# The tensor engine's products for an expert's slots beyond 128, under a compare-and-branch

## The chip, the cores and the metric

The kernel runs on one core of one Trainium2 chip. The metric is the device time of one execution in microseconds. Times are given as the median of three runs with the lowest and the highest beside it; the profile is one further execution, recorded by the hardware profiler.

The engines appear as the profile names them: PE is the tensor engine's matmul, PEld its weight load, DVE the vector engine, ACT the scalar engine, POOL GpSimd and SP the sync engine, which issues DMAs. A name with q at the end (ACTq, PEldq) is that engine's sequencer. PSUM is the memory in which PE accumulates.

## What is computed

The reference is two blocks of a language model, one after the other, on 512 tokens of 1024 values in fp32. The first block has two layers, and the second of them ends in a mixture of experts: eight experts of width 1536, two of them for each token.

```python
def moe_swiglu(h, router, w_gate, w_up, w_down):
    ...
    probs = jax.nn.softmax((ht @ router).astype(F32), axis=-1)
    top_p, top_i = lax.top_k(probs, TOP_K)
    top_p = top_p / jnp.sum(top_p, axis=-1, keepdims=True)
    ...
```

For each expert the tokens go through `silu(h @ w_gate) * (h @ w_up)` and then through `@ w_down`; a token's two results are added with the gates that the router gives. Here 512 tokens with two experts each make 1024 pairs, 128 for each of the eight experts on average; how many an expert really gets depends on the data. Everything else in the reference (the mixers, the dense feed-forward, the second block with its attention over a memory) is untouched by the change.

## The kernel before

The kernel is one program for all stages. A scheduler of the framework puts the instructions of a stage in an order for each engine and adds the semaphore waits that the data need; the source order around a stage is only its input. The stage in question is `moe` (line 1996), which runs from about 1063 to 1665 us of the profiled execution.

Ahead of it `dispatch` (line 1842) counts the tokens of each expert and gives each token its slots. An expert has `CAP` = 160 slots: 128 first ones, and 32 more for what goes beyond 128. A flag tells whether any expert has over 160; then, at the end of the program, a dense second computation replaces the result (under an `If`, line 2353; it is skipped here).

For expert `e`, `fetch` (line 2004) gathers the rows of its tokens with two indirect DMAs of POOL, `xa` (128 rows) and `xb` (32 rows). `turn` (line 2011) transposes them on PE. The 128 tokens are split in a high and a low part, `xh` and `xl`; the other 32 stay whole in `xs`.

Weights come in pieces through `weights` (line 2028). SP issues the DMA of a piece into `raw`, a ring of 8 buffers, ACT copies it to a rounded high part `wh`, and DVE subtracts to get the low part `wl`. A piece of the first product (gate and up) is 128×1536 fp32, 768 KB, and there are eight for each of two halves of an expert. A piece of the second product (down) is 128×1024, 512 KB, and there are twelve.

`block` (line 2036) does the 128 tokens for one piece with three products in a faster format: high by high, high by low, low by high. `few` (line 2045) does the other 32 tokens. It is called after every fourth piece (`FEW` = 4) and multiplies `xs` by the weights as loaded (`raw`), in fp32, four pieces at a time, with 16 matmuls in four groups of 32 columns of the array, into a PSUM tile `sec`. I call these 16 matmuls a section. In the trace a matmul in fp32 stands as two records, so a section is 32 records. A half (`gu`, line 2054) has two sections, a down product (`down`, line 2098) three: seven for an expert, 56 in all.

After the down product ACT and DVE copy the result out of PSUM into `y` (128 rows) and `ys` (the section's 32), and ACT's queue writes them to `ye` in memory, with one large transfer (line 2116) and four small ones (line 2118). After the last expert, indirect DMAs of POOL gather the rows of `ye` into `ya` and `yb` (line 2122). The hidden values are transposed for the down product by `turn_hid` (line 2079), with parts `th`, `tl` for the 128 tokens and `tsec` for the 32.

The loop of the stage runs over the experts: first half of expert e, down product of expert e-1, second half of expert e. The transposes are called from inside the loops over pieces, so that PE has them between matmuls.

The scheduler decides where a section stands in PE's stream. It spreads a section's matmuls between those of `block`, or puts them in one run.

Of the kernel before, what the change touches and what calls it, by code (L numbers as in the profile page):

```python
# [12 lines left out]
I32 = mybir.dt.int32  # L13
U32 = mybir.dt.uint32
AF = mybir.ActivationFunctionType
ALU = mybir.AluOpType
# [5 lines left out]
DFF, DFE, NE = 2816, 1536, 8  # L22
# [262 lines left out]
class Net:  # L285
# [72 lines left out]
    def sm(self, name, n):  # L358
        return self.M.tile([128, n], F32, name=name, tag="s_" + name, bufs=1)
# [1461 lines left out]
    def moe_init(self):  # L1821
        self.hd = self.D.tile([T, D], F32, name="hd")
        self.ye = self.D.tile([NE * CAP, D], F32, name="ye")
        self.flag = self.C.tile([1, 1], I32, name="flag")
        self.slot = self.C.tile([128, 2, 4], I32, name="slot")
        self.tokens = self.C.tile([128, 2, 8], I32, name="tokens")
        self.rp = self.C.tile([128, 2, 3, 4], F32, name="rp")
# [14 lines left out]
    def dispatch(self):  # L1842

        nc, F = self.nc, self.F
        tt, ts = nc.vector.tensor_tensor, nc.vector.tensor_scalar
        M_ = ALU.mult
        g = self.p("L1.n2")
        self.xg = []

        def chunk(c):  # L1850
            x = self.t("xg", "h")
            ts(x, self.X[c], g[:, c:c + 1], None, op0=M_)
            self.xg.append(x)
            F.set(0.6, "xg", c)

        sel, gates, r, _ = yield from self.route(g, lambda c: F.event("X", c), chunk)
        self.hrms = r
        sm, rp = self.rsm, self.rp

        pre, tot, fl = sm(4, 8), sm(8), sm(2)  # L1860
        nc.vector.memset(pre[:, 0], 0.0)
        for n in range(1, 4):
            tt(pre[:, n], pre[:, n - 1], sel[:, n - 1], op=ALU.add)
        tt(tot, pre[:, 3], sel[:, 3], op=ALU.add)
        yield F.event("sel")
        yield "px"
        pr = self.ps("px")
        pst = pr[:, 32:40]
        pr = pr[:, 0:32].rearrange("p (n e) -> p n e", n=4)
        self.pe.matmul(pr, self.const("tri128"), sel, start=True, stop=False)  # L1870
        self.pe.matmul(pr, self.const("ones"), pre, start=False, stop=True)
        self.pe.matmul(pst, self.const("ones"), tot, start=True, stop=True)
        st = sm(3, 4, 8)
        tt(st[:, 0], pr, sel, op=ALU.subtract)
        tt(st[:, 1], st[:, 0], self.const("ecap")[:, None, :].to_broadcast([128, 4, 8]), op=ALU.add)
        nc.vector.tensor_copy(st[:, 2], gates)

        big = self.t("rbig", "u")[:, :256].rearrange("p (n e f) -> p n e f", n=4, e=8)
        lt = self.const("lt8").rearrange("p (e f) -> p e f", e=8)[:, None].to_broadcast([128, 4, 8, 8])
        tt(big, sel[:, :, None, :].to_broadcast([128, 4, 8, 8]), lt, op=M_)  # L1880
        cnt, m, pk, ok = sm(4, 8), sm(4, 8), sm(3, 4, 8), sm(2, 4)
        nc.vector.tensor_reduce(cnt, big, axis=AX, op=ALU.add)
        at = self.t("slots", "u")[:, :CAP]
        nc.scalar.dma_start(at, self.A["slots"])
        oh, tid = [], []
        for k in range(2):
            ts(m, cnt, float(k), None, op0=ALU.is_equal)
            tt(m, m, sel, op=M_)
            tt(pk, st, m[:, None].to_broadcast([128, 3, 4, 8]), op=M_)
            nc.vector.tensor_reduce(rp[:, k], pk, axis=AX, op=ALU.add)  # L1890
            tid.append(sm(4, 8))
            tt(tid[k], m, self.const("tok")[:, :, None].to_broadcast([128, 4, 8]), op=M_)
            oh.append(self.t("oh", "B", (128, 4, CAP)))
            tt(oh[k], at[:, None, :].to_broadcast([128, 4, CAP]), rp[:, k, 0, :, None].to_broadcast([128, 4, CAP]),
               op=ALU.is_equal)
        F.rel("px", 2.0)
        yield 5.0
        yield "px"
        pi = self.ps("px")
        for o, w, c in ((0, 128, 0), (128, 32, 8)):  # L1900
            for q in range(8):
                k, n = q // 4, q % 4
                self.pe.matmul(pi[0:w, c:c + 8], oh[k][:, n, o:o + w], tid[k][:, n], start=q == 0, stop=q == 7)
        nc.vector.tensor_copy(self.tokens[:, 0], pi[:, 0:8])
        nc.vector.tensor_copy(self.tokens[0:32, 1], pi[0:32, 8:16])
        F.rel("px", 0.5)

        ts(ok, rp[:, :, 0], float(CAP), None, op0=ALU.is_lt)
        tt(ok, rp[:, :, 1], ok, op=M_)
        nc.vector.tensor_copy(self.slot, ok)  # L1910
        nc.vector.tensor_reduce(fl[:, 0:1], pst, axis=AX, op=ALU.max)
        ts(fl[:, 1:2], fl[:, 0:1], float(CAP), None, op0=ALU.is_gt)
        nc.vector.tensor_copy(self.flag, fl[0:1, 1:2])

    def rows(self):

# [79 lines left out]
    def moe(self, xin):  # L1996

        nc, A = self.nc, self.A
        ident = self.const("ident")
        tt, ts, act = nc.vector.tensor_tensor, nc.vector.tensor_scalar, nc.scalar.activation  # L2000
# [27 lines left out]
        def weights(src, n):  # L2028
            raw = self.t("raw", "rw", (128, 1536))[:, :n]
            hi, lo = (self.t(k, k, (128, 1536), F32R)[:, :n] for k in ("wh", "wl"))  # L2030
            nc.sync.dma_start(raw, src)
            self.wmark = act(hi, raw, AF.Copy)  # L2032
            tt(lo, raw, hi.bitcast(F32), op=ALU.subtract)  # L2033
            return raw, hi, lo
# [7 lines left out]
                self.pe.matmul(p, ah, lo[:, s], start=False, stop=False)  # L2042
                self.pe.matmul(p, al, hi[:, s], start=False, stop=last)

        def few(sec, todo, first, last):

            for i, (as_, raw) in enumerate(todo):
                q = raw.shape[1] // 4
                for b in range(4):
                    self.pe.matmul(sec[32 * b:32 * b + 32], as_, raw[:, q * b:q * b + q],  # L2050
                                   start=first and i == 0, stop=last and i == len(todo) - 1,
                                   tile_position=(0, 32 * b), skip_group_check=True)
            todo.clear()

        def gu(e, half, x, at=None):
            hi, lo, xs = x
            pg = [self.ps("pm")[:, :384] for _ in range(2)]
            pu = [self.ps("pf")[:, :384] for _ in range(2)]
            sec = self.ps("pf")[:, :384]
            todo = []  # L2060
            for k in range(8):
                w = weights(A["s_gu"][e, half, k], 1536)
                block(pg + pu, (hi[:, k], lo[:, k], xs[:, k]), w, 384, k == 0, k == 7)
                todo.append((xs[:, k], w[0]))
                if k % self.FEW == self.FEW - 1:
                    few(sec, todo, k < self.FEW, k == 7)
                if at and k in at:
                    at[k]()
            hid = self.t("hid", "hid", (128, 2, 384))
            for b in range(2):  # L2070
                sg = self.t("msg", "sg", (128, 384))
                act(sg, pg[b], AF.Silu)
                tt(hid[:, b], pu[b], sg, op=M_)
            hs, sg = self.t("hs", "hs", (128, 384)), self.t("msg", "sg", (128, 384))
            act(sg[64:128], sec[0:64], AF.Silu)
            tt(hs[64:128], sec[64:128], sg[64:128], op=M_)
            return hid, hs
# [21 lines left out]
        def down(e, T_, at=None):  # L2099
            th, tl, tsec = T_  # L2100
            ts_ = tsec.rearrange("p h b c s -> p (h b c) s")
            py, sec = [self.ps("px") for _ in range(2)], self.ps("px")[:, :256]
            todo = []
            for f in range(12):
                w = weights(A["s_dn"][e, f], D)
                block(py, (th[:, f], tl[:, f], ts_[:, f]), w, 512, f == 0, f == 11)
                todo.append((ts_[:, f], w[0]))
                if f % self.FEW == self.FEW - 1:
                    few(sec, todo, f < self.FEW, f == 11)
                if at and f in at:  # L2110
                    at[f]()
            y, ys = self.t("y", "y", (128, D)), self.t("ys", "ys", (128, 256))
            act(y[:, 0:512], py[0], AF.Copy)
            nc.vector.tensor_copy(y[:, 512:D], py[1])
            nc.vector.tensor_copy(ys, sec)
            nc.scalar.dma_start(self.ye[e * CAP:e * CAP + 128], y)
            for b in range(4):
                nc.scalar.dma_start(self.ye[e * CAP + 128:e * CAP + 160, 256 * b:256 * b + 256],
                                    ys[32 * b:32 * b + 32])
# [7 lines left out]
        for e in range(NE):  # L2127
            last = T_
# [253 lines left out]
```

## Time and profile before

| quantity | value |
|---|---|
| median of 3 runs | 2693.75 us |
| lowest and highest | 2688.41 and 2696.49 us |
| the profiled execution | 2687.84 us, its span 2686.1 us |
| PE busy over the span | 2560.9 us, 95% |
| DVE, ACT, POOL busy | 59%, 42%, 14% |
| mean DMA rate over the span | 134 GB/s |

The span is the time from the first to the last recorded instruction; the execution's own time is a little longer. Busy shares are means over stages with different limits. In the table of slices of the page, the slices of the mixture stage show PE at nine tenths or more nearly throughout, and DMA at seven to eight tenths, where most of the rest of the program has two or three. The parts to look at for this change are the stretches of that stage, single sections in the timeline, the landings of DMAs, and the places where PE stands.

### The profile page before, as it was taken

Reading aid. Unit: us, or ns where it says so; the run is one execution under the profiler, and the core shown is the slowest. Engines: PE = TensorE matmul, PEld = TensorE weight load, DVE = VectorE, ACT = ScalarE, POOL = GpSimd, SP = SyncE. Lnnn points to the kernel's source line nnn. Section 1 sums busy time; section 2 is a strip of 40 time slices with the busy share of each in tenths; the row PEclk is TensorE's granted clock in tenths of the full one; section 3 lists DMA queues with packets and bytes.
Section 4 is the critical chain, followed back from the end, with each engine's and each line's share of the span. In section 5 each row is a group of like instructions: output and inputs, shape, how many; then the busy total and the mean of one; then the engine's idle time right before and its main releaser. Section 6 shows DMA issues by size and latency. Waiting matters only on the chain.

```text
span 2686.1 us, 44080 instructions
## 1 busy us (share of the span) xinstructions
PE 2560.9 (95%) x18168; PEld 2012.0 (75%) x18168; DVE 1577.1 (59%) x2276; ACT 1126.1 (42%) x1608; POOL 366.9 (14%) x291
## 2 busy tenths in 40 slices
PE   7899999999989998999999998899989999999998
PEld 6787788888868677877777776676666676788887
DVE  6856743434575655766766675666744644544445
ACT  5344422223434534655555554553322334433332
POOL 3331000000343302000000001233432000000000
PEclk9999999999999998999999999999989999999999
DMA  3111322222311226787777776323233422222221
GB/s 117 55 57 41 90 91 95 94 94 96 117 56 62 65 81 214 271 317 282 289 268 280 267 269 234 126 69 104 87 112 111 158 90 66 92 94 94 94 94 57
DMA packets 102321, 359.40 MB, mean 134 GB/s; under 512 B 12384, under 2 KB 17888, under 8 KB 102112
## 3 DMA queue, kind: packets, MB, share of 16 engines
q1 hardware_dynamic: 81504, 305.32, 33.1%
q0 software_dynamic: 8128, 27.27, 2.9%
q10 hardware_dynamic: 12480, 23.91, 2.5%
q8 instruction: 145, 2.38, 0.4%
q14 instruction: 64, 0.52, 0.1%
HBM read 331.28 MB, written 25.17 MB: 133 GB/s over the span
## 4 chain that ended last, share of the span: by engine, by line
PE 56%; DVE 7%; issue 3%; ACT 2%; DMA 2%; POOL 0%; ACTq 0%; DVEq 0%; POOLq 0%
PE pm L278 34%; PE px L278 11%; PE pf L278 10%; PE px L282 1%; DVE ipr L480 1%; DVE cy L677 0%; DVE G L1587 0%; PE pf L282 0%; DMA ye<-ys 0%; DVE wlo L400 0%; DMA ya<-ye,slot 0%; DVE Tl L481 0%; DMA yb<-ye,slot 0%; ACT whi L398 0%; DVE rk L1592 0%
## 5 line engine op out<-in xcount | busy, mean ns | idle before, releaser
L398 ACT ACTIVATE whi<-raw 128x1024 fp32r<-128x1024 f32 (+5 forms) x304 | 297.6, 979 | 767.4 <-PE pm L278 525.9
L278 PE MATMUL pm<-xsh,whi 128*128 128x512 f32 x1280 | 530.0, 414 | 10.6 <-ACT xsh L372 4.8
L278 PE MATMUL pm<-xsl,whi 128*128 128x512 f32 x1280 | 511.6, 400 | 2.7 <-DVE xsl L373 2.7
L278 PE MATMUL pm<-xsh,wlo 128*128 128x512 f32 x1280 | 510.8, 399 | 2.7 <-POOL wlo L400 2.7
L2033 DVE TENSOR_TENSOR wl<-raw,wh 128x1536 fp32r<-128x1536 f32 (+1 forms) x224 | 341.6, 1529 | 132.8 <-PE pf L278 55.6
L2032 ACT ACTIVATE wh<-raw 128x1536 fp32r<-128x1536 f32 (+1 forms) x224 | 291.6, 1306 | 210.3 <-PE pf L278 96.6
L278 PEld LDWEIGHTS pm<-xsh,whi 128*128 128x128 f32 x1280 | 244.6, 191 | 87.2 <-issue 19.2
L278 PEld LDWEIGHTS pm<-xsh,wlo 128*128 128x128 f32 x1280 | 244.0, 191 | 62.8 <-POOL wlo L400 5.0
L278 PEld LDWEIGHTS pm<-xsl,whi 128*128 128x128 f32 x1280 | 244.8, 191 | 61.1 <-DVE xsl L373 5.3
L400 DVE TENSOR_TENSOR wlo<-raw,whi 128x1024 fp32r<-128x1024 f32 (+5 forms) x230 | 250.9, 1091 | 57.3 <-ACT whi L398 56.9
L400 POOL TENSOR_TENSOR wlo<-raw,whi 128x1024 fp32r<-128x1024 f32 x74 | 181.3, 2450 | 369.3 <-ACT whi L398 358.4
L278 PE MATMUL pm<-hidl,whi 128*128 128x512 f32 (+1 forms) x328 | 126.6, 386 | 0.0
L278 PE MATMUL pm<-hidh,wlo 128*128 128x512 f32 (+1 forms) x328 | 126.3, 385 | 0.0
L278 PE MATMUL pm<-hidh,whi 128*128 128x512 f32 (+1 forms) x328 | 125.9, 384 | 0.0
L1217 DVE TENSOR_TENSOR X<-X,pm 128x512 f32<-128x512 f32 x40 | 27.5, 688 | 119.8 <-PE pm L278 119.8
L278 PE MATMUL pm<-wh,xh 128*128 128x384 f32 x256 | 90.3, 360 | 6.9 <-ACT wh L2032 4.9
L278 PE MATMUL pf<-raw,xs 128*32 128x384 f32 x1024 | 95.8, 489 | 0.0
L278 PE MATMUL pm<-wl,xh 128*128 128x384 f32 x256 | 88.0, 344 | 4.4 <-DVE wl L2033 4.4
L278 PE MATMUL pm<-wh,xl 128*128 128x384 f32 x256 | 86.4, 338 | 0.0
L278 PE MATMUL pf<-wl,xh 128*128 128x384 f32 x256 | 86.1, 337 | 0.0
L278 PE MATMUL pf<-wh,xl 128*128 128x384 f32 x256 | 85.9, 336 | 0.0
L278 PE MATMUL pf<-wh,xh 128*128 128x384 f32 x256 | 84.8, 337 | 0.0
(623 smaller groups left out, 4794.0 us busy)
## 6 DMA issues: line engine op xcount, KB each, us to landing
raw<-in_s_gu_dram SPq DMA_DIRECT2D x128, 768.0 KB, 8.1
raw<-in_s_dn_dram SPq DMA_DIRECT2D x96, 512.0 KB, 5.5
raw<-in_f_gu_dram SPq DMA_DIRECT2D x44, 512.0 KB, 3.2
raw<-in_b_gu_dram SPq DMA_DIRECT2D x44, 512.0 KB, 3.2
raw<-in_b_wi_dram SPq DMA_DIRECT2D x38, 512.0 KB, 3.8
raw<-in_wq_dram SPq DMA_DIRECT2D x28, 512.0 KB, 3.6
raw<-in_f_dn_dram SPq DMA_DIRECT2D x16, 512.0 KB, 3.3
raw<-in_b_dn_dram SPq DMA_DIRECT2D x16, 512.0 KB, 3.2
```

The source lines that it names most:

```text
L278: return self.nc.tensor.matmul(o, l, r, **k)
L282: return self.nc.tensor.transpose(o, a, i)
L398: nc.scalar.activation(hi, raw, AF.Copy)
L400: (eng or nc.vector).tensor_tensor(lo, raw, hi.bitcast(F32), op=ALU.subtract)
L480: nc.vector.tensor_tensor(pr, A_, T_, op=ALU.mult)
L1217: nc.vector.tensor_tensor(self.X[m], self.X[m], ps, op=ALU.add)
L2032: self.wmark = act(hi, raw, AF.Copy)
L2033: tt(lo, raw, hi.bitcast(F32), op=ALU.subtract)
```

## The change

The router's stage computes one more thing: for each expert, whether its count exceeds 128. The eight flags go to registers of PE when the stage begins. Each section is put in a critical section of the scheduler (it stays in one piece, in one place), under a compare-and-branch of PE on the expert's flag. If the flag is zero, PE jumps over the 16 matmuls. As `sec` is then left unwritten, DVE clears it beforehand, once for each half and each down product.

```diff
+        self.many = self.C.tile([1, NE], I32, name="many")
...
         nc.vector.tensor_copy(self.flag, fl[0:1, 1:2])
+        over = sm(8)
+        ts(over, pst, 128.0, None, op0=ALU.is_gt)
+        nc.vector.tensor_copy(self.many, over[0:1])
...
-        def few(sec, todo, first, last):
-
+        PE = mybir.EngineType.PE
+        _, many = nc.values_load_multi_w_load_instructions(self.many[0:1, :], [PE], min_val=0, max_val=1)
+
+        def few(e, sec, todo, first, last):
+
+            with self.tc.tile_critical(no_gpsimd_drain=True):
+                with nc.tensor.If(many[e] > 0):
+                    few_rows(sec, todo, first, last)
+            todo.clear()
+
+        def few_rows(sec, todo, first, last):
             for i, (as_, raw) in enumerate(todo):
...
             sec = self.ps("pf")[:, :384]
+            nc.vector.memset(sec, 0.0)
...
             py, sec = [self.ps("px") for _ in range(2)], self.ps("px")[:, :256]
+            nc.vector.memset(sec, 0.0)
```

How this moves PE's instructions shows at two places. In the rows below `pm`, `pf` and `px` are PSUM tiles, and a name in brackets is a semaphore that the instruction waits for: DMAHW and DMASW are queues of DMAs, Activation is ACT, DVE, SP_sequencer and PE_sequencer are engines' and sequencers' own, and PE_49 is PE's.

The first place is PE's stream at the second half of expert 3, after the down product of expert 2, at the first four pieces. Before, the section's first matmul goes between two products of `block`, and the rest comes after the fourth piece, four at a time, each four waiting for its own piece:

```order
L278 MATMUL pm<-wh,xh 128x384 [waits Activation_49]
L278 MATMUL pm<-wh,xh 128x384
L278 MATMUL pf<-wh,xh 128x384 x2
L278 MATMUL pf<-raw,xs 32x384 [waits DMAHW3_49,PE_49]
L278 MATMUL pm<-wl,xh 128x384 [waits DVE_49]
...
L278 MATMUL pf<-raw,xs 32x384 x3
L278 MATMUL pf<-raw,xs 32x384 [waits DMAHW4_49]
L278 MATMUL pf<-raw,xs 32x384 x3
L278 MATMUL pf<-raw,xs 32x384 [waits DMAHW5_49]
```

With the change:

```order
L278 MATMUL pm<-wh,xh 128x384 [waits Activation_49]
L278 MATMUL pm<-wh,xh 128x384
L278 MATMUL pf<-wh,xh 128x384 x2
L2054 NO_OP [waits DMAHW1_49,DMAHW3_49,PE_sequencer_49,DMAHW4_49,DVE_49,Activation_49]
L2390 UNCONDITIONAL_BRANCH [waits DMASW5_49,DMASW6_49,DMASW4_49,DMASW7_49,DMASW3_49,DMAHW0_49,DMASW2_49,DMAHW1_49,DMASW1_49,DMAHW2_49,DMASW0_49,DMAHW3_49,SP_sequencer_49,DMAHW4_49,PE_sequencer_49,DMAHW5_49,DVE_49,DMAHW6_49,PE_49,DMAHW7
L2055 COMPARE_AND_BRANCH
L278 MATMUL pf<-raw,xs 32x384 x16
L2055 UNCONDITIONAL_BRANCH
L2054 NO_OP [waits PE_49,PE_sequencer_49]
L278 MATMUL pm<-wl,xh 128x384 [waits DVE_49]
```

All sixteen stand together now, after the high part of the second piece, and ahead of them PE waits for the DMA queues, the other engines and itself.

The second place is PE's stream at the start of the down product of expert 2, around its first section (pieces 0 to 3). Before, it comes after the fourth piece's last full matmul, with a wait for one piece's transfer ahead of each four:

```order
L278 MATMUL px<-wl,th 128x512
L278 MATMUL px<-wh,tl 128x512
L278 MATMUL px<-raw,tsec 32x256 [waits DMAHW7_49]
L278 MATMUL px<-raw,tsec 32x256 x3
L278 MATMUL px<-raw,tsec 32x256 [waits DMAHW0_49]
L278 MATMUL px<-raw,tsec 32x256 x3
...
L278 MATMUL px<-wh,th 128x512 [waits Activation_49]
```

With the change:

```order
L278 MATMUL px<-wh,th 128x512 [waits Activation_49]
L278 MATMUL px<-wh,th 128x512
L2054 NO_OP [waits DMAHW1_49,DMAHW2_49,DMAHW0_49,DMAHW7_49,PE_sequencer_49,DVE_49]
L278 MATMUL px<-wl,th 128x512 [waits DVE_49]
L2390 UNCONDITIONAL_BRANCH [waits DMASW5_49,DMASW6_49,DMASW4_49,DMASW7_49,DMASW3_49,DMAHW0_49,DMASW2_49,DMAHW1_49,DMASW1_49,DMAHW2_49,DMASW0_49,DMAHW3_49,SP_sequencer_49,DMAHW4_49,PE_sequencer_49,DMAHW5_49,DVE_49,DMAHW6_49,PE_49,DMAHW7
L2055 COMPARE_AND_BRANCH
L278 MATMUL px<-raw,tsec 32x256 x16
L2055 UNCONDITIONAL_BRANCH
L278 MATMUL px<-wh,tl 128x512
```

The section stands earlier, between the full matmuls of the second piece, and the waits for single pieces have become one wait for all queues and engines.

## Rows read from the trace of the kernel before

**Rows 1.** The page: busy time by engine; the chain that ended last.

```profile
PE 2560.9 (95%) x18168; PEld 2012.0 (75%) x18168; DVE 1577.1 (59%) x2276; ACT 1126.1 (42%) x1608; POOL 366.9 (14%) x291
...
PE 56%; DVE 7%; issue 3%; ACT 2%; DMA 2%; POOL 0%; ACTq 0%; DVEq 0%; POOLq 0%
```

**Rows 2.** Stretches: us, busy PE, PEld, DVE, ACT, POOL; clock; DMA share; GB/s.

```profile
1250.00:1350.00 100.00, 100.00 (x719) 79.23 (x719) 70.08 (x63) 57.29 (x57) 4.52 (x4) 1.00 0.76 282
```

**Rows 3.** Timeline of PE at a first-product section: start, us, instruction.

```profile
1086.96 0.33 PE L278 MATMUL pf<-wl,xh 128*128 128x384 f32 x1
1087.13 0.34 PE L278 MATMUL pf<-wh,xl 128*128 128x384 f32 x1
1087.40 2.79 PE L278 MATMUL pf<-raw,xs 128*32 128x384 f32 x32
1090.12 0.44 PE L278 MATMUL pm<-wh,xh 128*128 128x384 f32 x1
1090.40 0.33 PE L278 MATMUL pm<-wl,xh 128*128 128x384 f32 x1
```

**Rows 4.** Timeline of PE at a section of a down product.

```profile
1299.58 0.39 PE L278 MATMUL px<-wl,th 128*128 128x512 f32 x1
1299.81 0.39 PE L278 MATMUL px<-wh,tl 128*128 128x512 f32 x1
1300.12 1.93 PE L278 MATMUL px<-raw,tsec 128*32 128x256 f32 x32
1301.99 0.50 PE L278 MATMUL px<-wh,th 128*128 128x512 f32 x1
1302.33 0.40 PE L278 MATMUL px<-wl,th 128*128 128x512 f32 x1
```

**Rows 5.** Sequencer instructions of PE, by line: ns min/median/max, first and last start.

```profile
L2353 PEldq COMPARE_BRANCH  x1: 3735/3735/3735, 2676.3 to 2676.3; - x1
...
L282 PEldq EVENT_SEMAPHORE  x32: 51/51/51, 194.2 to 2246.5; - x32
...
L2344 PEldq TENSOR_LOAD <-flag x1: 487/487/487, 2675.7 to 2675.7; - x1
```

**Rows 6.** Timeline after a down product; landings of all `ye` transfers, then `ya`'s.

```profile
1307.33 0.39 PE L278 MATMUL px<-wh,tl 128*128 128x512 f32 x1
...
1309.34 0.34 ACTq L2116 DMA_DIRECT2D ye<-y  x1
...
1311.29 2.58 ACTq L2118 DMA_DIRECT2D ye<-ys  x4
...
DMA to landing us min/median/max: 1.6/8.0/9.3
...
DMA to landing us min/median/max: 8.6/9.2/9.3
```

**Rows 7.** Timeline at a second half's last section; landings of the `xb` gathers.

```profile
1259.62 0.90 POOL L2007 DMA_INDIRECT xb<-hd,tokens  x1 [0.30 <-PE pm L278]
...
1260.47 2.79 PE L278 MATMUL pf<-raw,xs 128*32 128x384 f32 x32
...
DMA to landing us min/median/max: 3.8/4.0/12.3
```

**Rows 8.** Landings of the `raw` transfers (line 2031); timeline of ACT, one split.

```profile
DMA to landing us min/median/max: 3.2/6.5/13.0
...
1260.57 1.49 ACT L2032 ACTIVATE wh<-raw 128x1536 fp32r<-128x1536 f32 x1 [0.51 <-PE pf L278]
```

**Rows 9.** A stretch at the start of the stage.

```profile
1060.00:1065.00 5.00, 3.38 (x33) 3.10 (x31) 0.61 (x2) 1.70 (x2) 1.66 (x2) 0.98 1.03 386
```

**Rows 10.** Timeline of PE at the last second half; the stretch behind it.

```profile
1623.09 0.69 PE L278 MATMUL pm<-wh,xh 128*128 128x384 f32 x1 [4.92 <-ACT wh L2032]
...
1626.19 0.69 PE L278 MATMUL pm<-wl,xh 128*128 128x384 f32 x1 [2.41 <-DVE wl L2033]
...
1626.00:1632.00 6.00, 5.81 (x20) 5.81 (x21) 3.12 (x3) 4.83 (x6) 0.00 (x0) 0.55 0.00 0
```

More of the change, by code (lines that the diff above doesn't have):

```diff
@@ L2052, in few @@
                                    tile_position=(0, 32 * b), skip_group_check=True)
-            todo.clear()
         def gu(e, half, x, at=None):
@@ L2065, in gu @@
                 if k % self.FEW == self.FEW - 1:
-                    few(sec, todo, k < self.FEW, k == 7)
+                    few(e, sec, todo, k < self.FEW, k == 7)
                 if at and k in at:
@@ L2108, in down @@
                 if f % self.FEW == self.FEW - 1:
-                    few(sec, todo, f < self.FEW, f == 11)
+                    few(e, sec, todo, f < self.FEW, f == 11)
                 if at and f in at:
```

## Prediction

> **What bounds the kernel now.** I read the page first: the tensor engine (PE) is busy for 95% of the span, and the chain that ended last lies on PE for 56% of its length [rows 1]. Then I read the mixture stage (1063 to 1665 us) by stretches. In its middle PE is busy for every one of 100 us at a granted clock of 1.00, VectorE for 70.08, ScalarE for 57.29, and the DMA engines for 0.76 of the time [rows 2]. So PE sets the end there, and a microsecond that PE neither works nor waits is a microsecond gained, until VectorE or the weight transfers become the bound. Nothing is waiting on anything else long enough to be seen, so a new wait of PE is paid in full.
>
> **What it removes.** For an expert with at most 128 tokens the products of the slots beyond 128 are skipped. A section on the first product (gate and up) holds PE from the start of the previous full matmul at 1087.13 to the next at 1090.12, 2.99 us, where full matmuls follow one another at 0.17; the next one is 0.11 longer than its peers. That is 2.92 us a section [rows 3]. On the second product (down) it is 1301.99 - 1299.81 = 2.18 less the cadence 0.22, plus a follower that is 0.11 to 0.12 late: 2.08 us [rows 4]. Each expert has four of the first and three of the second, 32 and 24 in all. Working the router out on the reference's inputs gives 122, 137, 122, 132, 129, 133, 127 and 122 tokens to the eight experts, so experts 0, 2, 6 and 7 skip: 16 × 2.92 + 12 × 2.08 = 46.7 + 25.0 = **71.7 us removed**. An expert that skips would then have some 53 us of PE work against some 50 us of VectorE work; VectorE would be late next, but PE is still first.
>
> **What it adds.** The order of the changed kernel shows that each of the 56 sections, skipped or not, is fenced. Ahead of its branch PE waits on every semaphore of the program at the last value given so far, PE's own among them: PE drains, and waits for weight transfers, gathers and result writes that have nothing to do with the section. Behind waiting PE stand all its full matmuls, and behind those VectorE and ScalarE. Behind the section there is a second drain. The terms:
>
> (a) *Drain and sequencer instructions, 56 times.* The trace has no such place. Nearest rows: a semaphore instruction of PE takes 51 ns [rows 5], and the last matmul of a row still runs 0.33 us after its start [rows 3]. Some dozen semaphore instructions and branches at 0.05, drain 0.33 twice less the cadence, and a restart make about 1.15 us: 64 us. Were most of them run ahead while matmuls are in flight, 0.4 us would stay (22); with twice the price for each instruction, 1.5 (84). I take 64, since a wait on PE itself lets nothing run ahead of it. [...] No row before shows a short untaken branch of PE.
>
> (b) *Result writes, 7 times.* The first section of the second half of each expert after the first now comes about 16 matmuls and 10 transposes, 4.1 us, after the last full matmul of the previous down product, and waits for all five of its writes. In the trace that matmul ends at 1307.7, the large write is issued at 1309.3 and the last of four small ones at about 1313.2 (5.5 us after), and writes land 1.6 to 9.3 us after issue, median 8.0 [rows 6]. So all have landed between 7.1 and 13.5 us after the matmul: a stall of 3.0 to 9.4 us. I take 5.4, nearer the lower end, because a standing PE frees no weight buffer and the queues empty: 6 × 5.4 = 32 (18 to 56). The seventh also waits for a gather of results (8.6 to 9.3 us to landing [rows 6]), some 12 us, but it replaces 4.92 + 2.41 us in which PE stands there already, with slow matmuls behind [rows 10]: +2.
>
> (c) *Token gathers, 5 times.* The last section of a second half waits for the gather of the expert two ahead. It starts 0.85 us before the section, and lands 4.0 us after its start (3.8 to 12.3) [rows 7]; 3.1 us late, less the fence: 5 × 2.8 = 14 (0 to 16).
>
> (d) *Weights that are prefetched, 24 times.* A section releases a raw buffer; the next fence waits for the transfer into it. Between two sections around the down product's start there are 8 matmuls at 0.22, 1.8 us; the shortest landing is 3.2, the median 6.5 [rows 8]. I take the end of a queue otherwise empty, 1.6 × 8 = 13 (0 to 38). The first section of a first half waits for ScalarE's split of the next weight, 1.49 us [rows 8]: 1.0 × 8 = 8. The section after it finds VectorE's product nearly done: 0.4 × 8 = 3. Together 24 (0 to 45).
>
> (e) *The start.* The first section of expert 0 waits for two weights more than now; at 386 GB/s [rows 9] 0.79 MB takes 2.0 us, so 3.5. The flags are loaded into registers before it: 0.49 us for one register [rows 5], eight at most 3.9, most of it in the 1.6 us of five in which PE stands at 1060 to 1065 [rows 9]: 1. Two VectorE operations and 24 clears of a PSUM tile lie on an engine with a third of its time free: 0, and if that cover went, under 0.5 us each, 12.
>
> (f) *The clock.* [...] Some seven matmuls each after the seven long stalls: 7 × 1.2 = 8 (0 to 25, for all the stalls over 2 us).
>
> Sum of costs: 64 + 32 + 2 + 14 + 24 + 4.5 + 8 = 148.5. Less 71.7: **+76.8 us**. The profiled run took 2687.84 us, so 2764.6; the median of the runs lies 5.9 above that run: **2770 us**, 2.9% slower.
>
> **Rivals.** *Fences that cost little (faster).* If the writes, gathers and weights have always landed when PE comes, and drain and sequencing are 0.5 us a section, the costs are 28 us: 2694 - 44 = 2650. For it: DMA is busy for only 0.76, and PE's queue could run ahead. Against it: [rows 6] and [rows 7], by which the landings are microseconds late at a dozen places. It decides where the whole cost of a section falls under 71.7 / 56 = 1.28 us.
>
> *No change.* Drains at 0.8 (45), the writes at their short end (18 + 2) and little of the rest (5) make 70: 2692. It needs three terms at their lower ends together.
>
> *A skipped section costs a fetch of code.* The one branch of PE before that jumps over much (the fallback at the end) took 3735 ns [rows 5]. If each of 28 taken branches paid that: +104, 2874. Against it: the target is 33 instructions ahead, where the fallback is a whole second computation. [...]
>
> *Nothing is skipped.* If the chip's counts were all above 128, the 71.7 would not be gained: 2842. The counts 127 and 129 are close, but 122 is not, and ties of the router are rare.
>
> **How the numbers follow.** Forecast 0.78; cheap fences 0.07; no change 0.07; code fetch 0.06; nothing skipped 0.02. A measurement here tells 0.3%, about 8 us, from no change. Faster 0.07, same 0.07, slower 0.86. Of the forecast's terms the distances to the lower ends (42, 14, 14, 24, 8) make 53 together, as independent errors, those to the upper (20, 24, 2, 21, 17) 42; with some slack 2710 to 2835. The range goes on to 2850 for the case where nothing is skipped, and leaves out 0.20.
>
> **What would show it.** In the profile after: in the mixture stage 28 sections without the 128×32 matmuls; PE busy falling below 90% there, and idle time ahead of the full matmul after each section. (a) is right if a fence in the middle of a down product leaves a hole of about 1.2 us; (b) if PE stands 4 to 6 us some 4 us into each second half, until a write of the results lands; (c) if it stands about 3 us at the last section of a second half until the gather lands; (d) if a hole of 1 to 2 us stands at the start of each down product; (f) if the clock drops behind (b). The forecast is wrong if the holes of (a) are near 0.5, or if the stalls of (b) and (c) don't show because the waits are met in another order than I read.

## The result, and the profile after

The changed kernel takes 2766.77 us (median of 4 runs, 2763.28 to 2770.09), the kernel before 2691.48. The ratio is 1.028, with an interval of 1.027 to 1.0296: 75 us slower. The forecast was 2770 us, within 2710 to 2850.

The profiled execution took 2763.28 us. Its page, busy time by engine:

```profile
span 2761.5 us, 43274 instructions
...
PE 2528.3 (92%) x17272; PEld 2007.1 (73%) x17272; DVE 1580.8 (57%) x2302; ACT 1126.3 (41%) x1608; POOL 368.1 (13%) x291
```

Against [rows 1] PE has 896 records fewer. That is 28 sections of 32: the half that the router's counts said. PE is busy 33 us less, and yet the span is 75 us longer. The loss is in idle time, which rose from 10 to 119 us in the stage, and in slow matmuls. A stretch of the stage's middle, with the columns of [rows 2]:

```profile
1250.00:1350.00 100.00, 82.20 (x490) 66.15 (x489) 63.10 (x59) 52.53 (x51) 2.92 (x2) 0.97 0.70 257
```

PE was busy for all of these 100 us, and is now for 82. VectorE, ScalarE and the DMA engines do less in the same time too: none of them took PE's place as the bound. Who ended PE's idle time in the stage (engine, line, what it waited for; us in total, times, longest):

```profile
PE pm L278 <- PEq L2054: 31.1, 18, 9.3
PE px L278 <- PEq L2054: 19.0, 23, 4.7
PE px L278 <- DMA raw<-in_s_dn_dram: 16.6, 8, 3.0
PE pf L278 <- issue: 9.0, 4, 4.0
```

PEq L2054 is PE's own sequencer at a section's fence. The third row is a weight transfer of the down product, which the fence of its first section waits for. In the last row the profile names no releaser.

A fence with nothing late to wait for looks like this where its section is skipped (timeline of PE):

```profile
1338.91 0.61 PE L278 MATMUL px<-wh,th 128*128 128x512 f32 x2
1340.61 0.47 PE L278 MATMUL px<-wl,th 128*128 128x512 f32 x1 [1.08 <-PEq L2054]
1340.92 0.39 PE L278 MATMUL px<-wh,tl 128*128 128x512 f32 x1
```

And like this where its section runs:

```profile
1416.50 0.61 PE L278 MATMUL px<-wh,th 128*128 128x512 f32 x2
1417.68 1.94 PE L278 MATMUL px<-raw,tsec 128*32 128x256 f32 x32 [0.57 <-issue]
1419.83 0.47 PE L278 MATMUL px<-wl,th 128*128 128x512 f32 x1 [0.21 <-PEq L2054]
```

The first costs about 1.2 us: the second matmul of its group starts 0.23 after 1338.91, the next matmul could start at 1339.37, and it starts at 1340.61. The second costs 2.87 us where the same section cost 2.08 before [rows 4], so 0.8 us. Both have the size that the prediction gave (a). Neither figure counts the matmul behind the fence, whose follower comes 0.31 us after it (1340.92) where 0.23 is usual.

What a fence looks like when something is late, at the gather for an expert two ahead:

```profile
1455.89 0.34 PE L278 MATMUL pm<-wh,xh 128*128 128x384 f32 x1
1460.18 5.35 PE L278 MATMUL pf<-raw,xs 128*32 128x384 f32 x32 [3.95 <-issue]
1465.63 0.44 PE L278 MATMUL pm<-wl,xh 128*128 128x384 f32 x1
```

PE stood for 3.95 us, and then the section itself took 5.35 us instead of 2.79 [rows 3]. The granted clock in that stretch is why:

```profile
1460.00:1466.00 6.00, 5.72 (x34) 1.81 (x35) 0.00 (x0) 0.22 (x1) 0.00 (x0) 0.54 0.01 3
```

0.54 is near half the clock, and the section took 1.9 times as long; the DMA engines moved almost nothing (3 GB/s): until the section is done, no weight buffer comes free, and the queues run dry. Half-clock time in the stage is 81.9 us, and PE is busy for 64.0 of it (before: 13.1 and 8.8).

At the start of the stage PE loads the flags (nanoseconds min/median/max, first and last start):

```profile
L2050 PEldq FUSED_REGOPS  x8: 146/146/160, 1042.4 to 1044.4; - x8
...
L2050 PEldq TENSOR_LOAD <-many x1: 1571/1571/1571, 1040.7 to 1040.7; - x1
```

### The profile page after: what moved, and what is told of

Its sections match the earlier page's. It is cut to its first block, busy times and chain, and to the rows that moved or that the text cites. A ratio compares the mean times of both kernels' runs of the same rounds, so it can differ in the third digit from the quotient of the medians.

```text
span 2761.5 us, 43274 instructions
## 1 busy us (share of the span) xinstructions
PE 2528.3 (92%) x17272; PEld 2007.1 (73%) x17272; DVE 1580.8 (57%) x2302; ACT 1126.3 (41%) x1608; POOL 368.1 (13%) x291
## 5 line engine op out<-in xcount | busy, mean ns | idle before, releaser
L278 PE MATMUL px<-wl,th 128*128 128x512 f32 x192 | 82.3, 429 | 22.2 <-PEq L2054 17.0
L278 PEld LDWEIGHTS pm<-wl,xh 128*128 128x128 f32 x256 | 49.6, 194 | 50.3 <-issue 30.2
```

Of the source, the lines that this page charges most:

```text
L278: return self.nc.tensor.matmul(o, l, r, **k)
```

## The experiments

**The skipped work alone.** The sections of experts 0, 2, 6 and 7 are left out when the program is written; of the rest of the change only the clearing of `sec` is there.

```diff
+        def few(e, sec, todo, first, last):
+            if e in (0, 2, 6, 7):
+                todo.clear()
+                return
```

> The kernel before, with the sections of experts 0, 2, 6 and 7 left out when the program is written (so it is right for these inputs alone), the section's PSUM tile cleared as in the change, and neither flags nor fences nor branches. Theory of the fences (the change loses by what stands around a section, and skipping is worth all of its 71.7 us): about 2692 - 72 = 2620 us. Rival (skipped work comes back, because VectorE, the weight transfers or the order become the bound): less than half of it is gained, 2655 us or more.

2644.73 us, ratio 0.983 (0.981 to 0.984): 47.5 us faster. That lies between the two expectations. So two thirds of the 71.7 us are there to be had in this kernel, if skipping costs nothing, and a third isn't. Where it stays can be seen in the stretches. The first two halves of expert 0, without sections:

```profile
1069.40:1089.70 20.30, 19.11 (x96) 17.66 (x96) 16.62 (x12) 13.90 (x12) 1.70 (x3) 0.93 1.02 393
1089.70:1110.30 20.60, 20.04 (x121) 19.01 (x122) 18.73 (x19) 15.75 (x16) 2.17 (x2) 1.00 1.02 415
```

They take 4.5 and 4.8 us less than before, not 5.84. The DMA engines are busy all of the time, and so is VectorE for most of it. At the last expert PE stands 8.3 us for the results' gather instead of 4.9 [rows 10]; with the idle time and the half clock behind it that place holds some 7 us more of the third. The rest of the third I could not place.

**Which of the two it is.** A quarter of the low-part splits of these halves was moved from VectorE to GpSimd.

```diff
-            tt(lo, raw, hi.bitcast(F32), op=ALU.subtract)
+            (nc.gpsimd.tensor_tensor if pool else tt)(lo, raw, hi.bitcast(F32), op=ALU.subtract)
...
+                w = weights(A["s_gu"][e, half, k], 1536, e in (0, 2, 6, 7) and k in (2, 5))
```

> The kernel with the sections of experts 0, 2, 6 and 7 left out at writing, which gained 48 us of the 72 that these sections hold PE; here two of the eight low-part splits of each of these experts' halves run on GpSimd instead of VectorE, 16 of 128 in all the first product's pieces and some 28 us of VectorE's time. If VectorE's splits are what full matmuls wait for in these halves: 2645 - 8 = 2637 us or less. If the weight transfers are (the DMA engines are busy all of the time in these stretches, at 393 to 415 GB/s): no gain, 2641 us or more, or a loss where PE waits for a GpSimd split.

2656.04 us: 11 us slower than without. But PE now waits for GpSimd's splits:

```profile
PE pm L278 <- POOL wl L2033: 22.7, 14, 5.4
```

These waits cover whatever VectorE gained, so this run does not tell the two apart. It stays open.

**Fences without the branch on the flag.** The order of work is that of the changed kernel.

```diff
             with self.tc.tile_critical(no_gpsimd_drain=True):
-                with nc.tensor.If(many[e] > 0):
-                    few_rows(sec, todo, first, last)
+                few_rows(sec, todo, first, last)
```

> The changed kernel with the fence of every section but without the compare-and-branch; all 56 sections run. PE's order is otherwise that of the changed kernel. Theory of the fences: the branch is a small part, so the time is the changed kernel's plus the 71.7 us of the 28 sections that run again, less about 0.45 us for each of these (in the changed kernel's trace a quiet fence costs 1.2 us where its section is skipped and 0.75 where it runs) and 0.15 us for each of 56 branches: 2767 + 72 - 13 - 8 = 2818 us. Rival (the branches themselves cost the time): 40 us or more below that, 2780 us or less.

2819.15 us, against 2818 expected: 127 us for 56 fences, with all work done and no branch on a flag. In its trace the 56 places hold PE for 259.9 us, where the 56 sections alone held it for 143.4 (32 × 2.92 + 24 × 2.08): 116.5 of the 127 us lie at the fences, and 3.35 at the loading of the flags. A fence keeps a branch of its own here (163 ns). No run has the sections in the changed order without fences, but little is left for the order.

**All sections run under the branches, and none.**

```diff
-        ts(over, pst, 128.0, None, op0=ALU.is_gt)
+        ts(over, pst, -1.0, None, op0=ALU.is_gt)
```

> The changed kernel with the flag set for every expert: all 56 branches fall through and all sections run. Theory of the fences: 2767 + 72 - 13 = 2826 us, and 8 us above the kernel with fences and no branch. Rival (a taken branch costs a fetch of code, microseconds each, which is in the changed kernel's time): this one would gain that back and stay under 2790 us.

2829.18 us, against 2826. It is 10 us above the kernel with fences only, or 0.18 us for each branch on a flag with its return; two medians can differ by nearly as much (0.3%, 8 us). The other extreme has the bound 160 in place of 128:

> The changed kernel with the flag set for no expert: all 56 branches are taken, and the tokens beyond 128 of four experts are left out. Theory of the fences: 2767 - 72 + 13 = 2708 us, so even a kernel that skips all of its sections is slower than the one before, which runs them all. Rival (each skip saves its section and the fences are a fixed loss that a larger share of skipped experts would pay back): 2767 - 72 = 2695 or less, level with the kernel before.

2731.45 us. So the first 28 skips give 62 us (2829 to 2767), the other 28 only 35. Even with nothing left to compute in the sections this kernel is 39 us slower than the one that computes all of them. My 2708 was too low by 23 us. Its trace shows 119.5 us at half clock in the stage, 98.0 of them with PE busy, where the changed kernel has 81.9 and 64.0: 34 us more of PE's work at half speed cost 17 of the 23 us. The branches by the records of the two kernels, first with none taken and then with all taken:

```profile
L2055 PEldq COMPARE_BRANCH  x56: 65/65/87, 1086.5 to 1795.8; - x56
```

```profile
L2055 PEldq COMPARE_BRANCH  x56: 202/208/378, 1082.2 to 1695.0; - x56
```

A taken branch lasts 0.14 us longer than one that falls through, far from the 3.7 us of [rows 5].

**The gathers off the fences.** The token gather of an expert is put behind a later fence in the program's order; its start still depends on its buffer alone.

```diff
+                if mark is not None:
+                    self.after(d, mark)
...
+            if e and e + 1 < NE:
+                late[4] = lambda: (turn_hid(hb, 1, last), box.update(nxt=fetch(e + 1, self.wmark)))
...
-            if e + 2 < NE:
-                nxt = fetch(e + 2)
```

> The changed kernel; the token gathers of an expert stand behind a later fence in the program's order (they still start as soon as their buffers are free), so that the last fence of a second half no longer waits for them. In the changed kernel's trace the five fences that wait for a gather cost 22 us beyond a quiet fence, slow matmuls behind them included. If the gathers set these waits: 2767 less some 20 = 2747 us. If something else at the same fences (the next weight, or ScalarE) comes nearly as late: 2760 us or more.

2755.8 us: 11 us gained, between the two. At the five fences themselves all was gained that the trace had promised: they hold PE for 15.8 us now, sections included, and did for 35.3. The gathers themselves start and land as before (one starts at 1203.4 us and takes 4.0 us, where it was 1203.5 and 4.0), so it was the waiting for them that cost the 19.5 us. But the eight loads of the residual, which had queued behind a gather at 1205 us, now ran from 1122 us on, beside the weights, and the fence in that stretch met a late weight:

```profile
1132.23 5.35 PE L278 MATMUL pf<-raw,xs 128*32 128x384 f32 x32 [6.21 <-DMA raw<-in_s_gu_dram]
```

That one place went from 4.35 to 11.82 us. So it seems that what was taken off came back there in part; no run has the residual's loads in their old place.

**One weight transfer off one fence.** On top of that, the fifth piece of each down product was put behind the fence of its first section.

```diff
+            if behind:
+                self.tc.add_manual_dep(d.ins, self.fence.name,
...
+                w = weights(A["s_dn"][e, f], D, f == 4)
```

> The kernel with the token gathers behind a later fence, and one more thing: the transfer of the fifth piece of every down product stands behind the fence of its first section in the program's order, so that this fence no longer waits for a transfer whose buffer has just come free. PE's order stays as it is. If that transfer sets the wait there (14 us in the changed kernel's trace, eight times): 2756 - 14 = 2742 us. If the split of the fourth piece, or the section's own weights, come as late: 2751 us or more. It also says whether the kernels with all weights behind the fences lost by the idea itself or by the other order of work that they got.

2747.55 us (2732.26 to 2750.67): 8 us gained where 14 were expected. Two medians can differ by as much, so the trace has to carry the reading. The fence in question, in the changed kernel:

```profile
1405.31 0.39 PE L278 MATMUL px<-wl,th 128*128 128x512 f32 x1
1407.91 1.94 PE L278 MATMUL px<-raw,tsec 128*32 128x256 f32 x32 [2.21 <-DMA raw<-in_s_dn_dram]
```

and in this one:

```profile
1394.38 0.39 PE L278 MATMUL px<-wl,th 128*128 128x512 f32 x1
1395.64 1.94 PE L278 MATMUL px<-raw,tsec 128*32 128x256 f32 x32 [0.86 <-ACT wh L2042]
```

The wait for the transfer is gone, and what remains is nearly a quiet fence. Over six of the eight down products the fences of the first sections gave back 12.0 us, and fences shortly after took 4.4 us of it.

**All weights off the fences.** Every weight transfer was put behind the fence ahead of its group, first alone, and then with all gathers.

```diff
+            behind(nc.sync.dma_start(raw, src))
```

> The changed kernel; every weight transfer stands behind the fence before it in the program's order (it still starts as soon as its buffer is free), so that a fence waits for no weights but those of its own section. The gathers are left as they are. If prefetched weights set the waits at the start of a down product, of a first half, and of the first expert (14 + 6 + 3 us in the changed kernel's trace): 2767 - 24 = 2743 us. If the fences were only waiting there for their own section's inputs: 2760 us or more.

> The changed kernel with weights, token gathers and result gathers all behind the next fence in the program's order; all 56 fences and branches stay. If the fences cost what they wait for, only the quiet ones are left (28 × 1.2 + 28 × 0.75 = 55 us and 3.5 us for the flags against 71.7 us of work skipped), and the clock drops less: 2692 - 72 + 58 + some 10 for the clock and for weights that now come late = 2688 to 2700 us. If drains and semaphore instructions are the larger part, as the prediction had it (64 us and the clock): 2715 us or more.

2818.06 and 2801.76 us, 51 and 35 us slower than the changed kernel. The times that the theory gave fell. The rivals' bounds (2760 and 2715 us or more) hold by their numbers alone, since the fences did become quiet: all 56 places hold PE for 144.5 us in the first kernel and 142.5 in the second, sections included, as much as all 56 sections held it before (143.4). The time went elsewhere, to the waits of PE between fences (in these rows PEq L2062 stands for the fences, the others for splits that come late):

```profile
PE pm L278 <- ACT wh L2044: 24.2, 13, 4.3
PE pm L278 <- PEq L2062: 21.5, 29, 4.0
PE px L278 <- DVE wl L2045: 12.8, 9, 1.6
PE pm L278 <- DVE wl L2045: 12.0, 15, 1.0
PE px L278 <- ACT wh L2044: 10.6, 10, 3.4
```

The dependency changed the order of the other engines too: a section now stands behind the last full matmul of its group, and at the end of each half ScalarE and VectorE do the activation and the transposes' copies before they split the first weight of the next group. PE meets unsplit weights at the boundaries: the four rows of late splits make 59.6 us, and in the changed kernel these kinds of wait make 11.3. So a wait was removed, and the overlap of the stage's halves with it. These two kernels don't measure the waits of the fences; the run with one transfer does.

**Fewer fences.** First 32 instead of 56, those of the first product, with the waits taken off as in the kernel above, then with the gathers off and the order left alone.

```diff
-                    few(e, sec, todo, f < self.FEW, f == 11)
+                    few_rows(sec, todo, f < self.FEW, f == 11)
+                    todo.clear()
```

> As the kernel with weights and gathers behind the fences, but the sections of the down products always run, without fence or branch, and the flags are loaded where PE waits for the tokens' transposes anyway. 32 quiet fences (16 × 1.2 + 16 × 0.75 = 31 us) against 16 × 2.92 = 47 us skipped: 2692 - 47 + 31 + some 5 = 2681 us, 0.4% faster than the kernel before. If a quiet fence costs more than its trace shows, or the skipped work comes back as waits for weights (as it did in part where sections were left out without fences): 2692 us or more.

> The changed kernel with 32 of its 56 fences: the down products' sections always run, without fence or branch; the token gathers stand behind a later fence, and the flags are loaded where PE waits for the tokens anyway. PE's order is near that of the changed kernel. Theory of the fences: 2756 (gathers off) + 25 (12 sections run again) - 23 (24 quiet fences) - 16 (the waits at the down products' fences) - 3 (flags) = 2739 us or a few less for the clock, still slower than the kernel before. If 24 fences fewer give back more than their own holes: 2715 us or less.

2772.48 and 2762.91 us, far from 2681 and 2739. The first is 29 us faster than its counterpart with 56 fences (2801.76), though 12 sections run again (25 us); the second is 7 us slower than its counterpart (2755.8), so 24 fences fewer, and the flags loaded elsewhere, gave back some 18 us where 42 were expected. In the second, the waits of PE say what took the place of the fences that went (the first row, ahead of transposes, is fences of skipped sections):

```profile
PE px L282 <- PEq L2053: 27.6, 6, 10.9
PE pf L278 <- DMA ye<-ys: 17.5, 4, 4.5
PE pf L278 <- DMA raw<-in_s_gu_dram: 14.7, 4, 6.6
```

The result writes `ye`, for which no fence waits in the changed kernel for long, hold PE here for 17.5 us at four fences of some 4.4 us. Without a fence in the down product they land later (the median of the large one is 8.8 us, where the changed kernel has 4.2), and PE meets them. Then only 16 fences, at places that are quiet in the changed kernel:

```diff
-                    few(e, sec, todo, f < self.FEW, f == 11)
+                    (few if f > 3 else plain)(e, sec, todo, f < self.FEW, f == 11)
...
-                    few(e, sec, todo, k < self.FEW, k == 7)
+                    plain(e, sec, todo, k < self.FEW, k == 7)
```

> The kernel before, with flags, fences and branches on the second and third section of each down product alone, 16 of 56, where the changed kernel's trace shows nothing late to wait for; all other sections run without fence or branch. By the trace's price of a quiet fence (1.2 us where its section is skipped, 0.75 where it runs), 8 × (1.2 - 2.08) + 8 × 0.75 + 3.5 for the flags: 2692 + 2.5 = 2694 us. If a quiet fence costs more than its own hole, since everything behind it comes later: 2705 us or more.

2758.02 us, with 16 fences: 67 us slower than before, where 2 were expected. The theory that a place has a price of its own fell. In this kernel the same places wait:

```profile
1327.24 0.49 PE L278 MATMUL px<-wl,th 128*128 128x512 f32 x1 [3.10 <-PEq L2054]
...
1338.06 1.00 PE L278 MATMUL pm<-wh,xh 128*128 128x384 f32 x2 [4.55 <-DMA raw<-in_s_gu_dram]
```

Here too a weight transfer ends a wait of 4.55 us. PE's idle time in the stage rose from 10 to 52 us for 16 fences. A second part is no wait at all. With the other sections free, the scheduler cut them up between full matmuls:

```profile
L278 PE MATMUL pf<-raw,xs 128*32 128x384 f32 x1024 | 120.8, 506 | 0.1
```

The same 1024 records took 95.8 us before, as this row of the kernel before shows, with the same columns (busy us, mean ns, idle before them); some 4 of the 25 us more are 42 records at half clock:

```profile
L278 PE MATMUL pf<-raw,xs 128*32 128x384 f32 x1024 | 95.8, 489 | 0.0
```

A likely reason why this kernel's fences meet late weights and the changed kernel's don't: an unfenced section gives its weight buffers back piece by piece until shortly before the next fence, and each release starts a transfer of at least 3.2 us [rows 8]; a fenced section gives all four back at once, some 7 us ahead of the next fence. This is read from the order and the traces; no run shows it.

No version with fences that does all the work came near the kernel before; the best has 2747.55 us.

## Why the prediction was right, step by step

The forecast missed the time by 3 us, but its terms by more: that the errors cancel so closely is luck. What holds is that the fences cost more than the skipped work, and most of the places where they do. The measured values are from the trace of the changed kernel, fence by fence; that of the first row is 28 sections at the prices of [rows 3] and [rows 4].

| term | predicted, us | measured, us |
|---|---|---|
| removed | -71.7 | -71.7 |
| (a) 56 quiet fences | 64 | 56 |
| (b) result writes, six | 32 | 3 |
| (b) the seventh | 2 | 2 |
| (c) token gathers | 14 | 16 |
| (d) prefetched weights | 24 | 20, and 5 at fences not named |
| (e) first fence | 3.5 | 3.4 |
| (e) flags | 1 | 3.5 |
| (f) clock | 8 | 28 |
| sum | 77 | 65 |

The two profiled runs differ by 75.4 us, so some 10 us are missing from the table. About half of them are the matmul behind each fence, whose follower comes some 0.08 us late (0.31 for 0.23 us, 0.25 for 0.17), 56 times: the table doesn't count it, while its first row takes the same lateness of 28 sections as saved. The rest I could not assign.

*Removed.* 28 sections went, as forecast. That each is worth its full time was right with fences for these 28 (62 us between none and half skipped, and 72 less 13 was expected), though not for the other 28 (35 us). It would have been wrong without fences: there it is 48.

*(a)* was sized well, at 1.2 and 0.8 us where 1.15 was taken for both, but that was luck too: it was added up from the wrong parts. The forecast let PE stand through a dozen semaphore instructions, since nothing would run ahead of the wait on PE itself. That was my estimate; no row showed it. There are eleven ahead of each section, and the fence has a branch of its own besides that on the flag:

```profile
L2390 PEldq EVENT_SEMAPHORE  x618: 51/51/9109, 1078.9 to 2761.4; - x155
L2390 PEldq COMPARE_BRANCH  x56: 169/169/307, 1084.7 to 1734.1; - x56
```

In the quiet fence at 1338.91 nine of the eleven start between 1337.84 and 1338.69, while full matmuls still run; in 36 of the 56 fences nine or ten do so before the last matmul has ended. What remains there is the end of that matmul, 0.16 us past the cadence, and 1.08 us: the fence's branch (0.17), the branch on the flag (0.21), a few short instructions, and about half a microsecond between them all. So most instructions did run ahead, for which the forecast would have had 0.4 us a fence, and the two branches and the spaces, at more than the 0.05 us taken, made up for it.

*(b)* is the term that failed. The place was read from the order and PE was there, but no write was late: in four of the six places all had landed before PE's last matmul ended, in the other two the last one lands 0.4 and 0.6 us after that, and a copy of ScalarE ends later still. The forecast had the writes land 9.5 us after the last full matmul and PE arrive 4.1 us after it. In the trace, for the down product of expert 2, the large write is issued 0.8 us after that matmul, not 1.6, since the earlier fence had let the small writes go first, and lands within 6.3; PE arrives after 5.9. The landings of the large write:

```profile
ye<-y ACTq DMA_DIRECT2D x8, 512.0 KB, 4.2
```

That is 4.2 us at the median, where it was 8.8 with PE hardly ever standing. Over all runs this goes with the fences of the down product: 3.5 to 5.5 us in the nine kernels that have them, 8.0 to 9.2 in the five that don't, the one with fences on the first product alone among them:

```profile
ye<-y ACTq DMA_DIRECT2D x8, 512.0 KB, 8.8
```

The forecast had a likely cause in hand (a standing PE empties the queues: in the six us from the issue of that write the DMA engines are busy for 0.75 of the time, before for 0.96) and used it for too little; no run shows the cause alone. That such writes can hold PE is shown by the same kernel, with 32 fences, where they do, some 4.4 us at a time.

*(c)* and *(d)* were right in place and nearly in size, and the runs confirm both causes. What the forecast did not see is that a wait taken off one fence comes back in part at the next: 19.5 us off the gathers' fences gave 11, 12 off those of the down products gave 8.

*(e)* The load of eight flags takes 1.57 us and their eight checks 0.28 us each, 4 us in all, and PE then stands for 3.34 us. I had hidden this behind an idle stretch 20 us later, which was idle for another reason. That the clears of `sec` cost nothing has no run of its own.

*(f)* is the second failed term. PE is busy for 64.0 us at half clock, 55 more than before, which costs half of that: 28 us, above the upper end of 25. I had charged the clock for the seven longest stalls only, and no run shows the seven matmuls, or 1.2 us, behind each. The trace shows half-clock stretches of 3.4 to 10.2 us at many shorter ones too, such as the 3.95 us above, and not only behind stops like the 4.92 us of [rows 10]. There, in the kernel before, full matmuls follow one another at 0.17 us ahead of the stop and at 0.32 behind it (1626.99 to 1630.84 us), at a granted clock of 0.55.

*The rivals.* Cheap fences: no; the 56 places cost (187.3 - 71.7) / 56 = 2.1 us each, from what they hold PE and what the kept sections held before, and it was to be decided at 1.28. No change: no. Code fetched for a taken branch, at 3.7 us: no; over 33 instructions it takes 0.2 to 0.4 us, at the median 208 ns taken and 65 ns untaken. Nothing skipped: no, 28 sections are gone.

## What to carry to other kernels

A branch around work on one engine is cheap here (0.07 to 0.2 us at the median, and 0.17 for the fence's own), but the fence that the framework puts around it waits for everything issued so far, prefetches included; so count the fences, and ask of each what was issued shortly ahead of it (the weight transfers of this stage land 5.9 to 6.9 us after issue at the median). Before building a gate, leave the gated work out by hand: here that gave 48 us of 72, and 56 fences, with the loading of the flags, cost 127. And when a sum comes out right, check its parts too: here the price of a quiet fence was right, and made of the wrong parts. When a dependency takes a wait away, compare the order of all engines afterwards, since a lost overlap can cost more than the wait, as it did with all weights off the fences (51 us).

## What had not been expected of the hardware

- A taken branch of PE over 16 matmuls takes 202 to 378 ns where all are taken, one that falls through 65 to 87 ns where none is.
- PE's semaphore instructions ahead of a fence run while its matmuls are still in flight: nine of eleven at the quiet fence at 1338.91 us.
- The register load of eight flags takes 1571 ns where one flag took 487 [rows 5].
- The five stops of PE of 3.9 to 4.5 us in the stage come with 3.4 or 6.8 us at half clock each, and with the 56 fences there are 69 us more of half clock in a stage of some 670 us.
- In the changed kernel, with fences in the down product, a write of 512 KB lands 4.2 us after issue at the median, where it took 8.8 in the kernel before.
